# A hybrid DeltaNet, attention and FFN block: attention halves scaled in PSUM, decayed keys in 128-row tiles, FFN-down sums a stage ahead

## The chip, the cores and the metric

One core of a Trainium2 chip runs the whole program in one launch. The metric is the device time in microseconds (us), the median of several executions. The engines are named as in the profile: PE (TensorE matmul), PEld (its weight loads), DVE (VectorE), ACT (ScalarE), POOL (GpSimd), SP (SyncE, which issues the transfers).

## The reference

One layer on x of 1 x 1024 x 1024 (sequence, model width), all in float32:

```python
h = rmsnorm(x, norm_mix_w)
qa, ka, va, za, ba, aa, qb, kb, vb, ga, gb = split(h @ w_in)
# mixer A, 4 heads of 128: causal conv of 4 taps and SiLU on q, k, v, l2-norm of q and k,
# then per chunk of 64 positions, with G = cumsum(g), gam = exp(G):
w, uv = solve(I + beta*(k k^T)*dec_strict, [beta*gam*k, beta*v])   # unit lower triangular, 64 x 64
kd    = k * exp(G_last - G)                                        # decayed keys
def step(s, (w, uv, p, qg, kd, gl)):
    u = uv - w @ s
    o = qg @ s + p @ u
    s = gl * s + kd^T @ u                                          # state, 128 x 128
oa = rmsnorm(o) * silu(za)
# mixer B, 8 heads of 64: banded attention, a chunk sees itself and 8 chunks before, with relative bias
ob = softmax(0.125 * qb kb^T + bias) vb
x = x + (sigmoid(ga)*(oa @ w_branch_a) + sigmoid(gb)*(ob @ w_branch_b)) @ w_out
g, u = split(causal_dwconv3(rmsnorm(x) @ w_up) + b)                # 2 x 2816
out = rmsnorm(x + (silu(g)*u) @ w_down)
```

## The kernel before, in words

A float32 product is made of three faster ones (type fp32r): both operands are split into a high and a low half, and `hi*hi + hi*lo + lo*hi` are summed in PSUM. For weights `load_w` (L84) has SP load a tile `wraw`, ACT cast `whi` (L81) and POOL subtract `wlo` (L82). The normed input lies in SBUF as `BH` and `BL`. A *half* of a projection is 128 output channels by 512 positions: 8 k-tiles x 3 = 24 matmuls of 128x512 into one PSUM tile `psph`, all issued by `mm` (L52). There are two of these buffers (`psP`).

The stages follow each other: input norm and first projections (to about 60 us), DeltaNet (60 to 455), attention (455 to 745), mixing of the branches (745 to 845), `w_out` and the second norm (to 940), FFN up in Strassen-Winograd form (940 to 1350), FFN down in the same form, to the end.

DeltaNet, per head: `gdn_prep` (L400) transposes the keys into PSUM (`psk`), copies them to `nKs`, writes the decayed keys `Kd` (scaled by `eg[:, 2]`, L431) and sums squares (`jk`, `ssk`, L433, L434) for the norm `rk`. `gdn_prep2` (L441) makes the 64x64 matrices and scales `nKs` and `Vs` in place (L487, L488). The triangular system is solved in 31 steps on DVE (L506, L508) and its result, which goes through DRAM, is applied (`gdn_apply`, `psW`, `psU`, U). Then `gdn_chain` goes through 16 chunks, in 8 tiles p of two chunks e each:

```python
mm(ps, WQ[:, p, e * P:(e + 1) * P], S, start=True, stop=True)         # psws, 128 rows
nc.vector.tensor_add(U[r, p, :], ps[r], U[r, p, :])                   # r: rows of chunk e
mm(ps2, Kd[r, p, :], U[r, p, :], start=True, stop=True)               # pss, 64 rows
S2 = S * eg + ps2                                                     # DVE, L574
```

After each second chunk comes `pso`. These float32 matmuls take two passes each, and both stand in the trace as instructions. Projections of the next head and halves of the gates fill PE in between: the tables in L33 to L40 count, per head, how many tiles of the chain are emitted before which part of the next head (C1, C2, C3), how many halves go before `gdn_apply` and the q norm (APP, APK, QN), and how many gate halves are filled in (GFILL; 32 in all, 22 of them in DeltaNet). A scheduler then orders each engine's queue by priorities; `behind` puts work behind a named instruction.

A gate (`gate`, L166) takes two halves: DVE multiplies by the norm's factor into `gt`, ACT applies tanh, SP stores it. What is left of the gates after DeltaNet is woven into the last attention pair, 8 halves of it, and the rest runs behind it, ahead of the mixing. The mixing wants `oh`, `ol` (DeltaNet's output, from DRAM) and `bh`, `bl` (attention's, from `obT`), each cast by ACT and subtracted by DVE (`load_oa`, `split`).

Attention goes in four pairs of heads. `att_qkv` (L754) makes v, q and k in halves: `scaled` multiplies `psph` by the norm's factor into an SBUF tile `u` (two buffers, L768); ACT writes `Q` or `Kh` from it, DVE the low parts (`Q<-u,Q` L777, `Kl<-u,Kh` L787). v is transposed (`psvt`, in the same two PSUM buffers). `att_pair` makes scores (`pss`), softmax (`Sb`, `ast`), transposes (`psp`, `PTh`, `PTl`) and products with V (`pso`); each pair is woven with the projections of the next, the first pair's projections stand alone.

FFN up works on pairs of blocks with seven products P1 to P7 (`pa`, `pb`, `pc`, `pd` are PSUM tiles, `q` a sum in SBUF); DVE forms the sums that later products accumulate on (`sum_q`, `sum_pc`). FFN down goes through the seven products in the order P1, P5, P6, P3, P7, P2, P4, each 11 steps of 12 matmuls; `prep_w` (L1471) makes the weights of two steps at a time: DVE's sums `W<-W,W` for the two steps after, ACT's casts `wdh`, DVE's `wdl`; POOL or DVE splits the activations (`al`).

Of the kernel before, what the change touches and what calls it, by code (L numbers as in the profile page):

```python
# [8 lines left out]
F32 = mybir.dt.float32  # L9
# [26 lines left out]
APP = (10, 10, 10, 2)  # L36
APK = (7, 4, 3, None)
QN = (7, 3, 4, 5)
PR0 = 1
GFILL = (4, 4, 5, 5, 4)  # L40
# [6 lines left out]
def hybrid_kernel(ctx: ExitStack, tc: tile.TileContext, a):  # L47
# [176 lines left out]
    def first_rms(e):  # L224

        s = slice(e * HN, (e + 1) * HN)
        psr = psa.tile([P, HN], F32, tag="a", name="psrb")
        for i in range(4):
            xt = gp.tile([P, D], F32, tag=("Kd", "U")[i % 2], name="xt", bufs=2)
            nc.sync.dma_start(xt, a["x"][(4 * e + i) * P:(4 * e + i + 1) * P, :])  # L230
            ssq = sml.tile([P, 1], F32, tag="ssq", name="ssq")
            nc.scalar.activation(xt, xt, AF.Square, accum_out=ssq)
            ms = sml.tile([P, 1], F32, tag="ms", name="ms")
            nc.vector.tensor_scalar(out=ms, in0=ssq, scalar1=1.0 / D, scalar2=EPS, op0=ALU.mult, op1=ALU.add)
            rs = sml.tile([P, 1], F32, tag="rs", name="rs")
# [32 lines left out]
    wraw, whi, wlo = (gw.tile([P, KT, P], dt, tag=tg, name="wv") for dt, tg in ((F32, "sq"), (F32R, "nKs"), (F32R, "Vs")))  # L268
# [131 lines left out]
    def gdn_prep(c):  # L400
# [13 lines left out]
        Kd = gp.tile([P, NT, P], F32, tag="Kd", name="Kd", bufs=2)  # L414
# [8 lines left out]
        for e in range(2):  # L423
# [6 lines left out]
            for i in range(4):  # L430
                nc.scalar.activation(Kd[:, 4 * e + i, :], pks[e][:, i, :], AF.Copy, scale=eg[:, 2, 4 * e + i, h:h + 1])  # L431
            for i in range(4):
                nc.scalar.activation(jk, nKs[:, 4 * e + i, :], AF.Square, accum_out=ssk[:, 4 * e + i:4 * e + i + 1])  # L433
        nc.vector.tensor_scalar_add(ssk, ssk, EPS)  # L434
# [6 lines left out]
    def gdn_prep2(c):  # L441
# [19 lines left out]
        nc.scalar.activation(decT.rearrange("p n j -> p (n j)"), psd2, AF.Exp)  # L461
# [24 lines left out]
        for p in range(NT):  # L486
            nc.scalar.activation(nKs[:, p, :], nKs[:, p, :], AF.Copy, scale=nks[:, p:p + 1])  # L487
            nc.scalar.activation(Vs[:, p, :], Vs[:, p, :], AF.Copy, scale=bv[:, p:p + 1])  # L488
# [34 lines left out]
    def gdn_apply(c):  # L523
# [17 lines left out]
        U = gp.tile([P, NT, P], F32, tag="U", name="U", bufs=2)  # L541
# [14 lines left out]
    def gdn_chain(c):  # L556
# [6 lines left out]
        for p in range(NT):  # L563
            for e in range(2):
# [7 lines left out]
                mm(ps2, Kd[r, p, :], U[r, p, :], start=True, stop=True)  # L572
# [22 lines left out]
    def gdn_qnorm(c):  # L595

        sqq = gw.tile([P, NT, P], F32, tag="sq", name="sqq")
        nc.scalar.activation(sqq, c["WQ"][:, :, 64:192], AF.Square)
        psn = psc.tile([P, 8], F32, tag="c", name="psn")
        for p in range(NT):  # L600
            side.append(lambda p=p: mm(psn[:, p:p + 1], sqq[:, p, :], ones, start=True, stop=True))
        c["psn"] = psn
# [151 lines left out]
    def att_qkv(pr, c):  # L754
# [9 lines left out]
        def scaled(w, e):  # L764

            ps, s = proj_half(w, BH, BL, KT, e)
            u = ap_.tile([P, HN], F32, tag="u", name="u", bufs=2)
# [34 lines left out]
        for e in range(2):  # L802
            vT[e], s = scaled(w, e)
            yield
# [539 lines left out]
    prs[1].P2(True)  # L1344
    sub(BL[:, k1, s], b22, BH.bitcast(F32)[:, k1, s])
# [25 lines left out]
    p, r = prs  # L1371
    p.P5()
    p.sum_q()
    p.sum_pa()
    r.sum_pa()
    p.P6()
    p.sum_pc()
# [93 lines left out]
    def prep_w(k):  # L1471

        n = min(2, NS - 2 * k)
        for s in range(2 * k + 2, min(2 * k + 4, NS)):
            w_sum(s)
# [325 lines left out]
```

## Time and profile before

| | us |
|---|---|
| three runs | 1590.27, 1591.93, 1592.96 |
| median | 1591.93 |
| the profiled execution | 1592.53 |
| its span, first to last instruction | 1590.6 |
| PE busy | 1542.7 (97%) |
| DVE busy | 1120.3 (70%) |
| ACT busy | 698.0 (44%) |
| POOL busy | 595.6 (37%) |
| mean granted clock of PE | 0.994 |

Busy PE is a modelled figure for pipelined matmuls; what the tables below show as idle, with the instruction whose end released it, is the time in which PE had nothing to do. Operations of the FFN's helper all carry one line (L1155), so there the tiles tell them apart. In fp32r a projection matmul starts every 0.227 us at the full clock (2.4 GHz) and half as often at the lower level (1.2 GHz).

### The profile page before, as it was taken

The page shows a single profiled execution, that of the slowest core. Times are in us where ns is not written, and L with a number is a line of the kernel's source. Part 1 is how long each engine was busy: PE and PEld are TensorE (multiplying, and loading weights), DVE is VectorE, ACT ScalarE, POOL GpSimd, SP SyncE. Part 2 cuts the span into 40 slices and gives each one's busy share as a digit, 9 for nine tenths or more (in the row PEclk, how much of TensorE's full clock was granted, in tenths as well). Part 3 has the DMA queues.
Part 4 walks back from the last instruction along what each step waited for, and adds up shares of the span by engine and source line. Part 5 has one row for each costly group of instructions (what it writes and reads, how often), then busy time and mean ns, then how long its engine had stood idle before and what let it go on. Part 6 is the DMA issues. An engine that isn't in the chain of part 4 may idle for free.

```text
span 1590.6 us, 21158 instructions
## 1 busy us (share of the span) xinstructions
PE 1542.7 (97%) x7687; PEld 1255.8 (79%) x7687; DVE 1120.3 (70%) x2150; ACT 698.0 (44%) x1376; POOL 595.6 (37%) x449
## 2 busy tenths in 40 slices
PE   8999999999999999999999999999999999999997
PEld 6777776877777787888887887888888888788885
DVE  6795867948436878875665566777777777787787
ACT  7535334352225655654222244444444444433344
POOL 2422212212131101110220148877777776233353
PEclk9999999999999999999999999999999999999998
DMA  7021121122131101122654222233332332775533
GB/s 294 27 73 59 56 73 38 46 77 68 60 123 48 32 26 44 36 73 81 194 167 139 90 80 86 90 114 111 115 108 100 100 100 74 246 245 172 177 93 139
DMA packets 74504, 162.03 MB, mean 102 GB/s; under 512 B 15648, under 2 KB 16928, under 8 KB 74400
## 3 DMA queue, kind: packets, MB, share of 16 engines
q1 hardware_dynamic: 74400, 160.68, 30.5%
q8 instruction: 60, 0.98, 0.3%
q14 instruction: 44, 0.36, 0.1%
HBM read 120.55 MB, written 40.11 MB: 101 GB/s over the span
## 4 chain that ended last, share of the span: by engine, by line
PE 49%; DVE 3%; DMA 2%; ACT 1%; issue 1%; SPq 0%; POOL 0%; POOLq 0%; DVEq 0%; ACTq 0%
PE psph L52 8%; PE pb L52 7%; PE psd L52 7%; PE psout L52 5%; PE pc L52 5%; PE pa L52 4%; PE pb L1141 4%; PE psd L1493 3%; PE pc L1141 2%; PE pa L1141 2%; DMA araw<-dA 1%; DVE yu L1155 1%; PE pso L52 0%; DMA oaT<-dO 0%; DVE wdl L1155 0%
## 5 line engine op out<-in xcount | busy, mean ns | idle before, releaser
L82 POOL TENSOR_TENSOR wlo<-wraw,whi 128x1024 fp32r<-128x1024 f32 (+1 forms) x57 | 120.2, 2108 | 464.7 <-ACT whi L81 259.5
L52 PE MATMUL psph<-BH,whi 128*128 128x512 f32 x688 | 280.4, 408 | 10.1 <-ACT BH L220 5.2
L52 PE MATMUL psph<-BH,wlo 128*128 128x512 f32 x688 | 275.9, 401 | 1.7 <-POOL wlo L82 1.7
L52 PE MATMUL psph<-BL,whi 128*128 128x512 f32 x688 | 277.4, 403 | 0.0
L52 PEld LDWEIGHTS psph<-BH,whi 128*128 128x128 f32 x688 | 130.8, 190 | 34.8 <-ACT BH L220 5.9
L1155 POOL TENSOR_TENSOR ol<-wraw,oh 128x512 fp32r<-128x512 f32 x110 | 150.6, 1386 | 9.1 <-ACT oh L1155 9.1
L52 PEld LDWEIGHTS psph<-BH,wlo 128*128 128x128 f32 x688 | 130.8, 190 | 26.0 <-POOL wlo L82 2.1
L52 PEld LDWEIGHTS psph<-BL,whi 128*128 128x128 f32 x688 | 130.7, 190 | 23.1 <-DVE BL L221 1.0
L52 PE MATMUL psd<-wdl,ah 128*128 128x512 f32 (+1 forms) x311 | 121.6, 391 | 5.4 <-DVE wdl L1155 5.4
L1155 POOL TENSOR_TENSOR al<-araw,ah 128x1024 fp32r<-128x1024 f32 (+1 forms) x28 | 70.5, 2518 | 143.7 <-ACT ah L1155 143.6
L1155 POOL TENSOR_TENSOR wraw<-wraw 128x512 f32<-128x512 f32 x86 | 119.5, 1389 | 4.9
L1493 PE MATMUL psd<-wdh,al 128*128 128x512 f32 (+1 forms) x311 | 121.1, 390 | 0.0
L52 PE MATMUL psd<-wdh,ah 128*128 128x512 f32 (+1 forms) x311 | 119.8, 389 | 0.0
L1155 ACT CAST oh<-wraw 128x512 fp32r<-128x512 f32 x110 | 67.8, 621 | 102.0 <-POOL wraw L1155 101.9
L1155 DVE TENSOR_TENSOR wdl<-W,wdh 128x512 fp32r<-128x512 f32 x77 | 88.4, 1186 | 30.7 <-ACT wdh L1155 30.7
L1155 ACT CAST ah<-araw 128x1024 fp32r<-128x1024 f32 (+1 forms) x39 | 40.6, 1041 | 115.9 <-issue 48.8
L81 ACT CAST whi<-wraw 128x1024 fp32r<-128x1024 f32 (+2 forms) x61 | 55.4, 908 | 78.9 <-PE psph L52 55.1
L1155 POOL TENSOR_TENSOR gl<-wraw,gh 128x512 fp32r<-128x512 f32 x42 | 55.9, 1332 | 69.6 <-ACT gh L1155 69.6
L52 PEld LDWEIGHTS psd<-wdl,ah 128*128 128x128 f32 x311 | 58.8, 189 | 20.0 <-DVE wdl L1155 7.9
L1141 PE MATMUL pa<-BH,gh 128*128 128x512 f32 x176 | 68.6, 389 | 0.0
L52 PE MATMUL pa<-BH,gl 128*128 128x512 f32 x176 | 68.5, 389 | 0.0
L52 PE MATMUL pa<-BL,gh 128*128 128x512 f32 x176 | 68.5, 389 | 0.0
(342 smaller groups left out, 3826.2 us busy)
## 6 DMA issues: line engine op xcount, KB each, us to landing
wraw<-w_up SPq DMA_DIRECT2D x44, 512.0 KB, 4.9
wraw<-w_tiles SPq DMA_DIRECT2D x42, 512.0 KB, 3.5
araw<-dA SPq DMA_DIRECT2D x77, 256.0 KB, 3.0
dA<-yu SPq DMA_DIRECT2D x33, 512.0 KB, 3.1
W<-w_down SPq DMA_DIRECT2D x44, 256.0 KB, 4.7
xt<-x SPq DMA_DIRECT2D x16, 512.0 KB, 5.0
dG<-gt SPq DMA_DIRECT2D x16, 512.0 KB, 2.8
ta<-dG SPq DMA_DIRECT2D x16, 256.0 KB, 2.7
```

What stands on the lines that cost most here:

```text
L52: last["mm"] = nc.tensor.matmul(*args, **kw).ins
L81: nc.scalar.copy(hi, src)
L82: (eng or nc.gpsimd).tensor_tensor(out=lo, in0=src, in1=hi.bitcast(F32), op=ALU.subtract)
L1141: i = nc.tensor.matmul(ps, wh[:, k], xh[:, k], start=start and k == 0, stop=False, **kw)
L1155: return lambda *args, **kw: tc.keep_in_program_order(f(*args, **kw))
L1493: i = nc.tensor.matmul(ps, al[:, j, ts], wh[:, es], start=False, stop=stop, **kw)
```

## The change

Names and places (line numbers of before):

- `Kd` is a pair of persistent tiles [128, 8, 2, 128], zeroed by POOL at the start; the rows of chunk e lie in slot e, the other half stays zero. They are written in `gdn_prep2` from `nKs` instead of in `gdn_prep` from PSUM, as 16 ACT operations of 64 rows per head instead of 8 of 128 rows, and `pss` contracts all 128 rows.
- `ssk` gets its epsilon on POOL instead of DVE; some temporary tiles share other buffers.
- The tables APP, APK, QN and GFILL change: 24 gate halves in DeltaNet instead of 22.
- In attention q's and k's halves are scaled in place in `psph`; only v's go to `u`.
- At the FFN's start two products and their sums are emitted ahead of the last splits of the input.
- In FFN down the sums for P4 are made in the P2 stage.

```diff
-APP = (10, 10, 10, 2)
-APK = (7, 4, 3, None)
-QN = (7, 3, 4, 5)
+APP = (11, 10, 10, 2)
+APK = (2, 4, 3, None)
+QN = (7, 5, 7, 5)
 PR0 = 1
-GFILL = (4, 4, 5, 5, 4)
+GFILL = (6, 4, 5, 5, 4)
...
+    Kds = []
+    for i in range(2):
+        t_ = gp.tile([P, NT, 2, P], F32, name=f"Kd{i}")
+        nc.gpsimd.memset(t_, 0.0)
+        Kds.append(t_)
...
-        Kd = gp.tile([P, NT, P], F32, tag="Kd", name="Kd", bufs=2)
+        Kd = Kds[h % 2]
...
             nc.scalar.copy(nKs[:, 4 * e:4 * e + 4, :], pks[e])
             for i in range(4):
-                nc.scalar.activation(Kd[:, 4 * e + i, :], pks[e][:, i, :], AF.Copy, scale=eg[:, 2, 4 * e + i, h:h + 1])
-            for i in range(4):
                 nc.scalar.activation(jk, nKs[:, 4 * e + i, :], AF.Square, accum_out=ssk[:, 4 * e + i:4 * e + i + 1])
-        nc.vector.tensor_scalar_add(ssk, ssk, EPS)
+        nc.gpsimd.tensor_scalar_add(ssk, ssk, EPS)
...
-        nc.scalar.activation(decT.rearrange("p n j -> p (n j)"), psd2, AF.Exp)
+        last["exp"] = nc.scalar.activation(decT.rearrange("p n j -> p (n j)"), psd2, AF.Exp).ins
...
-        for p in range(NT):
-            nc.scalar.activation(nKs[:, p, :], nKs[:, p, :], AF.Copy, scale=nks[:, p:p + 1])
-            nc.scalar.activation(Vs[:, p, :], Vs[:, p, :], AF.Copy, scale=bv[:, p:p + 1])
+        Kd = c["Kd"]
+        with behind("exp"):
+            for p in range(NT):
+                for e in range(2):
+                    r = slice(e * CH, (e + 1) * CH)
+                    nc.scalar.activation(Kd[r, p, e, :], nKs[r, p, :], AF.Copy, scale=eg[r, 2, p, h:h + 1])
+                nc.scalar.activation(nKs[:, p, :], nKs[:, p, :], AF.Copy, scale=nks[:, p:p + 1])
+                nc.scalar.activation(Vs[:, p, :], Vs[:, p, :], AF.Copy, scale=bv[:, p:p + 1])
...
-        U = gp.tile([P, NT, P], F32, tag="U", name="U", bufs=2)
+        U = gp.tile([P, NT, P], F32, tag="U", name="U")
...
-                mm(ps2, Kd[r, p, :], U[r, p, :], start=True, stop=True)
+                mm(ps2, Kd[:, p, e, :], U[:, p, :], start=True, stop=True)
...
-        def scaled(w, e):
+        def scaled(w, e, out=False):
             ps, s = proj_half(w, BH, BL, KT, e)
-            u = ap_.tile([P, HN], F32, tag="u", name="u", bufs=2)
+            u = ap_.tile([P, HN], F32, tag="u", name="u", bufs=2) if out else ps
             nc.vector.tensor_mul(u, ps, rb[:, s])
             return u, s
...
-            vT[e], s = scaled(w, e)
+            vT[e], s = scaled(w, e, True)
...
     prs[1].P2(True)
+    p, r = prs
+    p.P5()
+    p.sum_q()
+    p.P6()
+    p.sum_pc()
     sub(BL[:, k1, s], b22, BH.bitcast(F32)[:, k1, s])
     sub(hf[:, k1], hf[:, k1], tf[:, k1])
     vsplit(hf[:, k1], BH[:, k0, s], BL[:, k0, s])
...
-    p, r = prs
-    p.P5()
-    p.sum_q()
     p.sum_pa()
     r.sum_pa()
-    p.P6()
-    p.sum_pc()
     p.gate_a()
...
         for s in range(2 * k + 2, min(2 * k + 4, NS)):
-            w_sum(s)
+            if plan[s // FH][0] == "P2":
+                w_sum(s + FH)
+            elif plan[s // FH][0] != "P4":
+                w_sum(s)
```

PE in the first pair of attention, behind the second `psvt`: before (its next `psph` is the second half of q).

```order
L52 MATMUL psph<-BH,wlo 128x512
L792 MATMUL psvt<-ident,u 128x128 [waits DVE_49,PE_49]
L792 MATMUL psvt<-ident,u 128x128 x3
L52 MATMUL psph<-BH,whi 128x512 [waits DVE_49]
L52 MATMUL psph<-BL,whi 128x512
```

The same place now.

```order
L52 MATMUL psph<-BH,wlo 128x512
L802 MATMUL psvt<-ident,u 128x128 [waits DVE_49]
L802 MATMUL psvt<-ident,u 128x128 x3
L52 MATMUL pss<-Kh_4358,Q_4356 128x256 [waits Activation_49]
L52 MATMUL pss<-Kh_4358,Q_4356 128x256
L52 MATMUL pss<-Kl_4360,Q_4356 128x256 [waits DVE_49]
L52 MATMUL pss<-Kl_4360,Q_4356 128x256
L52 MATMUL psph<-BH,whi 128x512 [waits DVE_49,PE_49]
```

Four scores moved ahead of that half, and its first matmul now waits for PE's and DVE's work on the half that used the buffer before.

PE at the end of the last attention pair, before: the last gate half (`BH`), then the first half of the mixing, whose `oh` of k-tile 3 and `bh` are cast last.

```order
L52 MATMUL psph<-BH,wlo 128x512
L52 MATMUL psph<-oh_6420,whi 128x512 [waits DVE_49]
L52 MATMUL psph<-ol_6421,whi 128x512
L52 MATMUL psph<-oh_6420,wlo 128x512 [waits Pool_49]
L52 MATMUL psph<-oh_6426,whi 128x512
L52 MATMUL psph<-ol_6427,whi 128x512
L52 MATMUL psph<-oh_6426,wlo 128x512
L52 MATMUL psph<-oh_6432,whi 128x512
L52 MATMUL psph<-ol_6433,whi 128x512
L52 MATMUL psph<-oh_6432,wlo 128x512
L52 MATMUL psph<-oh_7177,whi 128x512 [waits Activation_49]
L52 MATMUL psph<-ol_7178,whi 128x512 [waits DVE_49]
```

The same place now, right behind the last `pso` of the pair.

```order
L52 MATMUL pso<-PTl_4351,V 128x256
L52 MATMUL psph<-oh_6504,wlo 128x512
L52 MATMUL psph<-oh_6510,whi 128x512
L52 MATMUL psph<-ol_6511,whi 128x512
L52 MATMUL psph<-oh_6510,wlo 128x512
L52 MATMUL psph<-oh_7193,whi 128x512 [waits Activation_49]
L52 MATMUL psph<-bh_7199,whi 128x512 [waits Activation_49]
L52 MATMUL psph<-ol_7194,whi 128x512 [waits DVE_49]
L52 MATMUL psph<-oh_7193,wlo 128x512
L52 MATMUL psph<-bl_7203,whi 128x512 [waits DVE_49]
L52 MATMUL psph<-bh_7199,wlo 128x512 [waits Pool_49]
L52 MATMUL psph<-bh_7200,whi 128x512 [waits Activation_49]
```

No gate half stands between the last `pso` and the mixing any more, and the first two halves of the mixing take turns.

DVE at the FFN's start, before.

```order
L1155 TENSOR_TENSOR XT3l<-tf,XT3h 128x4x128 [waits Activation_49]
L1155 TENSOR_TENSOR BL<-pst,BH 128x4x128
L1155 TENSOR_TENSOR hf<-hf,tf 128x512
L1155 TENSOR_TENSOR BL<-hf,BH 128x4x128 [waits Activation_49]
L1155 TENSOR_TENSOR q<-pc,p_8611 128x512 [waits PE_49]
L1155 TENSOR_TENSOR pa<-pa,p_8611 128x512
L1155 TENSOR_TENSOR pa<-pa,p_8700 128x512
L1155 TENSOR_TENSOR pc<-pb,q 128x512 [waits DVE_49,PE_49]
```

The same place now.

```order
L1165 TENSOR_TENSOR XT3l<-tf,XT3h 128x4x128 [waits Activation_49]
L1165 TENSOR_TENSOR q<-pc,p_8627 128x512 [waits PE_49]
L1165 TENSOR_TENSOR pc<-pb,q 128x512 [waits DVE_49,PE_49]
L1165 TENSOR_TENSOR BL<-pst,BH 128x4x128
L1165 TENSOR_TENSOR hf<-hf,tf 128x512
L1165 TENSOR_TENSOR BL<-hf,BH 128x4x128 [waits Activation_49]
L1165 TENSOR_TENSOR pa<-pa,p_8627 128x512
L1165 TENSOR_TENSOR pa<-pa,p_8716 128x512
```

`q` and `pc` moved ahead of `BL`, `hf`, `BL` and the two `pa`.

## Rows read from the trace of the kernel before

**Rows 1.** Page, part 1: busy us and share of the span by engine.

```profile
PE 1542.7 (97%) x7687; PEld 1255.8 (79%) x7687; DVE 1120.3 (70%) x2150; ACT 698.0 (44%) x1376; POOL 595.6 (37%) x449
```

**Rows 2.** Windows in DeltaNet: us, busy time (x instructions) by engine, granted clock, DMA share, GB/s.

```profile
160.00:180.00 20.00, 19.49 (x92) 14.11 (x91) 17.26 (x42) 5.74 (x14) 3.25 (x6) 1.00 0.17 53
415.00:455.00 40.00, 39.09 (x187) 28.20 (x186) 22.81 (x63) 8.53 (x25) 5.66 (x3) 1.00 0.11 40
```

**Rows 3.** Instruction groups, PE, 60 to 460: count, busy, mean ns, idle before.

```profile
L52 PE MATMUL pss<-U,Kd 64*128 64x128 f32 x128 | 31.6, 327 | 4.5 <-DVE U L569 4.5
L52 PE MATMUL psws<-S,WQ 128*128 128x128 f32 x128 | 25.5, 281 | 1.4 <-DVE S L574 1.4
```

**Rows 4.** Timeline, PE, chain of the first head: start, us, line, matmul, tile.

```profile
176.88 0.39 PE L52 MATMUL psph<-BL,whi 128*128 128x512 f32 x1
177.12 0.38 PE L52 MATMUL psws<-S,WQ 128*128 128x128 f32 x2
...
177.57 0.40 PE L52 MATMUL psph<-BH,whi 128*128 128x512 f32 x1
177.81 0.40 PE L52 MATMUL psph<-BL,whi 128*128 128x512 f32 x1
178.13 0.48 PE L52 MATMUL pss<-U,Kd 64*128 64x128 f32 x2
...
178.88 0.39 PE L52 MATMUL psph<-BH,whi 128*128 128x512 f32 x1
```

**Rows 5.** Timeline, DVE, the same chain.

```profile
174.95 0.29 DVE L569 TENSOR_TENSOR U<-psws,U 64x128 f32<-64x128 f32 x1
...
176.22 0.34 DVE L574 SCALAR_TENSOR_TENSOR S<-S,eg,pss 128x128 f32<-128x128 f32 x1
...
177.54 0.28 DVE L569 TENSOR_TENSOR U<-psws,U 64x128 f32<-64x128 f32 x1 [0.48 <-PE psws L52]
```

**Rows 6.** Instruction groups, ACT, 60 to 455.

```profile
L431 ACT ACTIVATE Kd<-psk,eg 128x128 f32<-128x128 f32 x32 | 10.1, 390 | 0.0
```

**Rows 7.** Timeline, ACT and DVE, end of attention.

```profile
747.36 3.91 ACT L81 CAST bh<-obT 128x1024 fp32r<-128x1024 f32 x4
...
748.52 3.50 DVE L82 TENSOR_TENSOR bl<-obT,bh 128x1024 fp32r<-128x1024 f32 x3 [0.72 <-ACT bh L81]
```

**Rows 8.** Timeline, DVE and POOL, a woven pair of attention.

```profile
552.41 0.55 DVE L867 TENSOR_TENSOR PTl<-psp,PTh 128x384 fp32r<-128x384 f32 x1
552.88 1.94 DVE L787 TENSOR_TENSOR Kl<-u,Kh 64x512 fp32r<-64x512 f32 x1
...
554.91 0.69 DVE L787 TENSOR_TENSOR Kl<-u,Kh 64x512 fp32r<-64x512 f32 x1
...
551.86 2.41 POOL L82 TENSOR_TENSOR wlo<-wraw,whi 128x1024 fp32r<-128x1024 f32 x1 [9.40 <-PE psp L862]
```

**Rows 9.** Timeline, PE in attention: rows with idle time and its releaser.

```profile
499.77 0.33 PE L862 MATMUL psp<-ident,Sb 128*128 128x128 f32 x1 [1.70 <-DVE Sb L851]
...
544.43 0.76 PE L862 MATMUL psp<-ident,Sb 128*128 128x128 f32 x5 [1.78 <-DVE PTl L867]
```

**Rows 10.** Timeline, first pair: PE where k's and q's halves begin, ACT's copies.

```profile
476.30 0.47 PE L52 MATMUL psph<-BH,whi 128*128 128x512 f32 x1 [0.87 <-DVE u L768]
...
482.78 0.50 PE L52 MATMUL psph<-BH,whi 128*128 128x512 f32 x1 [0.35 <-DVE u L768]
...
484.80 0.62 ACT L786 CAST Kh<-u 64x512 fp32r<-64x512 f32 x1
```

**Rows 11.** FFN start: timeline of PE, and window 960 to 970.

```profile
962.27 0.50 PE L1141 MATMUL pb<-XT3h,oh 128*128 128x512 f32 x1 [2.11 <-DVE pc L1155]
...
960.00:970.00 10.00, 7.89 (x28) 6.22 (x28) 6.41 (x10) 4.39 (x7) 8.47 (x8) 0.83 0.50 154
```

**Rows 12.** Timeline, PE and DVE, last stage of down.

```profile
1567.51 0.50 PE L52 MATMUL psd<-wdl,ah 128*128 128x512 f32 x1 [2.45 <-DVE wdl L1155]
...
1563.37 3.48 DVE L1155 TENSOR_TENSOR W<-W,W 128x512 f32<-128x512 f32 x2
```

More of the change, by code (lines that the diff above doesn't have):

```diff
@@ L228, in first_rms @@
         for i in range(4):
-            xt = gp.tile([P, D], F32, tag=("Kd", "U")[i % 2], name="xt", bufs=2)
+            pool, tag = ((gp, "U"), (gp, "Lr"), (gw, "vf"))[i % 3]
+            xt = pool.tile([P, D], F32, tag=tag, name="xt")
             nc.sync.dma_start(xt, a["x"][(4 * e + i) * P:(4 * e + i + 1) * P, :])
@@ L267, in hybrid_kernel @@
     nc.vector.tensor_scalar_mul(nea, nea, -1.0)
-    wraw, whi, wlo = (gw.tile([P, KT, P], dt, tag=tg, name="wv") for dt, tg in ((F32, "sq"), (F32R, "nKs"), (F32R, "Vs")))
+    wraw, whi, wlo = (gw.tile([P, KT, P], dt, tag=tg, name="wv") for dt, tg in ((F32, "kf"), (F32R, "nKs"), (F32R, "Vs")))
     nc.sync.dma_start(wraw, a["w_tiles"][2 * GH])
@@ L595, in gdn_qnorm @@
     def gdn_qnorm(c):
-        sqq = gw.tile([P, NT, P], F32, tag="sq", name="sqq")
+        sqq = gp.tile([P, NT, P], F32, tag="zs", name="sqq")
         nc.scalar.activation(sqq, c["WQ"][:, :, 64:192], AF.Square)
```

## The prediction

> **What bounds the kernel now.** I read the page's busy shares first, then the granted clock by stretch, then what ends TensorE's idle time, and last the timelines around those places. TensorE (PE) is busy 97% of the span, VectorE (DVE) 70% [rows 1]: so the time is PE's work plus PE's holes, and an edit counts only if it takes passes from PE, closes a hole, or opens one. The profiled execution took 1592.53 us for a span of 1590.6; it lies 0.6 us above the median of the runs, 1591.93. I make the sum against 1592.5 and take 0.6 off at the end. A change of under 0.2% (3.2 us) can hardly be told from none here.
>
> In DeltaNet PE is nearly full (19.49 of 20 us, 39.09 of 40), but DVE is not far behind in some stretches: 17.26 of 20 us at 160 to 180, only 22.81 of 40 in the last head [rows 2].
>
> **Decayed keys in 128 rows.** The state update `pss` contracts 64 rows before, 128 after (the other 64 are zeros). Its passes have the longest mean of the chain, 327 ns against 281 for `psws`, which has the same 128 columns and contracts 128 rows [rows 3]. The timeline tells more. From one projection matmul at 176.88 to the second one after it, at 177.57, with a `psws` pair between them, are 0.69 us; from 177.81 to 178.88, with a `pss` pair between, 1.07 us [rows 4]. Without a pair two projection steps take 2 x 0.23 = 0.46. So a `psws` pair costs PE 0.23 and a `pss` pair 0.61: the change of shape costs time going in and coming out. There are 128 `pss` passes, 64 pairs: 64 x 0.38 = **24.3 us** is the most that can go. The Trainium skill ("TensorEngine Tiling (Array Packing)", When to Use Tiling) advises row tiling for a contraction of 64, which speaks against this edit; its Key Properties add that a switch of mode drains the engine, and that is what these rows show for a lone tile among full ones. By the first rule alone this edit would save nothing.
>
> How much of 24.3 survives? The chain is a loop PE, DVE (U), PE, DVE (S). Its step is 2.59 us from one U to the next [rows 5]. The loop's own time I estimate at 1.7 us: the `psws` pair 0.38 + U 0.28 + the `pss` pair about 0.45 + S 0.34 + some 0.25 for four hand-overs [rows 4, 5]. A step shortened by 0.38 is 2.2, so the loop itself does not bind, and in all chains PE waited for U only 4.5 us and for S 1.4 [rows 3]. But where DVE is busy 17.26 of 20 us [rows 2], taking seven steps x 0.38 = 2.7 us out leaves it no air, and each U or S then stands behind somebody's 0.7 us operation. I take **-18** (bounds 0 and -24.3; the value lies nearer the upper end, since the last head has a DVE at 57% [rows 2] and the small waits for U and S speak for room in the others).
>
> **Preparing a head.** Eight ACT copies per head, 390 ns each [rows 6], go from the path to `ssk`, and sixteen come in later, behind the exponential of `decT`. ACT has room; what can suffer is a conv activation queued behind the now 32-long block (about 0.39 x 16 = 6 us more at worst, of which the fill hides all but 0 to 2 us a head). The sum of `ssk` moves to POOL, which then no longer waits for DVE's queue; nothing of PE hangs on that. The two zero fills on POOL at the start lie before its first work. The renamed buffers I cost at nothing: U of the next head is written after the previous chain has ended. Together **-1** (from -2.5 to +4).
>
> **Gate halves.** Two gate halves (48 matmuls, 10.9 us of PE at 0.227) move from behind the last attention pair into DeltaNet. As work they cost the same. But there they were cover: they ran while ACT cast the four `bh` (3.91 us) and DVE made the `bl` (3.50 for three) [rows 7]. In the changed order PE has 4 matmuls left after the last `pso` and then wants `oh`, `bh`, `ol`, `bl` in turn. ACT needs about 1.0 us each, DVE 1.17 for `ol` and each `bl`, starting one cast later: 0.6 + 1.0 + 5 x 1.17 + 0.5 = 7.9 us until the last is used, against 19 matmuls x 0.227 = 4.3. What is late next is `bl`: **+3.5** (0 to +6).
>
> **Queries and keys in PSUM.** Gain: DVE's Q and Kl operations read two SBUF operands now. `Kl` takes 1.94 us while POOL computes `wlo` (2.41 us, from 551.86), and 0.69 after it [rows 8]; `PTl`, in the middle of the same `wlo` but with an operand in PSUM, takes 0.55. So with `psph` in place of `u` I expect about 0.7 beside POOL too. The price of it now is PE waiting for what DVE does next: 1.78 us at 544.43 [rows 9]. Three such holes of 1.8 (one a woven pair), three of about 1.1 behind the second of k's halves, and one of 1.70 in the first pair make 10.3 us. The Trainium skill ("VectorE: DVE Perf Modes", Rules for kernel authors) would copy to SBUF first when many operations follow; the rows (0.55 and 0.69 with either source) give no reason to.
>
> Cost: the accumulator is held until its last reader. There are two such buffers, shared with `psvt`. In the first pair, where nothing is woven in, k's first half follows q's first half on the same buffer. Today it starts at 476.30 after 0.87 idle [rows 10]. The idle time began at 475.43, behind a `psvt` of about 0.6, so q's last matmul ends near 474.8. After: hand-over 0.2, scaling 0.69, one copy for Q, one for V and one more for Q on ACT (0.62, some 0.4, 0.62) and DVE's last Q 0.69 make 478.0: +1.7. The second half of q waits for four ACT copies (0.62 each, the last from 484.80) and the last Kl: about 3.0 idle in place of 0.35 [rows 10], +2.7. In woven pairs the scores, transposes and value products of the pair before lie between the halves, and I add 1.5 for all of it, half-clock stretches included. Together -10.3 + 4.4 + 1.5 = **-4.4** (from -10 to +8).
>
> **FFN start.** `q` and `pc` come ahead of three other operations on DVE. Now PE waits 2.11 us for `pc`, and the granted clock of the ten microseconds from 960 is 0.83 [rows 11]: 10 x 0.17 = 1.7 us lost to the lower level (1.2 of 2.4 GHz) after that hole. `pc` can be ready 2 to 3 us sooner, both should go: **-3.5** (-3.8 to 0; the displaced BL is then late by some tenths).
>
> **Down.** The sums for P4 move a stage ahead. PE's hole of 2.45 us ends at 1567.51 on a `wdl` that stood behind two sums, 3.48 us [rows 12]; a part stays, since `wdl` itself has two SBUF operands beside POOL's `al`. The P2 stage now has these sums, in front of its own `wdl`: where a pair falls beside POOL's work it costs 3.48 there too, and a new hole of 1 to 2 us is likely. **-3** (-5 to +1).
>
> **Sum:** -18 - 1 + 3.5 - 4.4 - 3.5 - 3 = -26.4; 1592.5 - 26.4 = 1566.1, less 0.6: **1565.5 us**; with the spread of the terms 1557 to 1573.
>
> **Rivals.** (1) *DVE takes over in the chains.* For: the 17.26 of 20 us. Against: 5.9 us of waits for U and S in four heads. Then 18 shrinks to about 8: 1575.5 (1573 to 1583). Chance 0.15. (2) *Held accumulators (slower).* Place: each half of k and the second half of q, two a pair, eight waits. Should the woven work not cover them either, each costs 3.0 us of idle and the 1.7 us of lower clock that followed a hole of 2.1: 8 x 4.7 = 38, and the -10.3 is not seen. The other terms give -22, so it decides from 2.75 us a wait on; at 4.7 the time is 1592 - 22 + 38 = 1608 (1595 to 1610). Against: PE's rows between the halves in woven pairs. Chance 0.05. (3) *128 rows cost what 64 do,* because the passes next to them, not the shape, make the 0.61: no saving in the chains, 1583.5. The rule on row tiling of the skill's page would have it so. Against: `psws` in the same neighbourhood. Chance 0.06, with 0.03 of it within 0.2% when the holes stay as well. (4) *All holes close and the chains give the full 24:* 1550 to 1557. Chance 0.16.
>
> **How the numbers follow.** The forecast's own case has 0.55, rival 1 0.15, rival 2 0.05, rival 3 0.06, rival 4 0.16, and 0.03 stays for other losses around 1585. The range 1553 to 1580 leaves out rivals 2 and 3, the ends of 1 and 4: under 0.2. Faster: 0.92; same 0.03; slower 0.05.
>
> **What would show it.** Right: `pss` as a 128*128 pass with a mean near 280 ns, and two projection steps around it in 0.69; PE's work in DeltaNet shorter by some 14 us net of the added halves; Q and Kl at about 0.7 each; no wait for `pc` at the FFN's start and a clock of 1.0 behind it. Wrong: PE idle before `pss` or `psws` summing to over 15 us (rival 1), PE idle before `psph` in woven pairs with Kl or Q as releaser (rival 2), `pss` still at 0.6 a pair (rival 3). New holes I expect at k's and q's halves in the first pair, before `bl`, and in P2.

## The result and the profile after

The changed kernel takes 1574.3 us (median of four runs, 1572.72 to 1575.6), the kernel before 1592.33 in the runs beside it. The ratio is 0.9889, interval 0.9871 to 0.9906: 18 us faster, inside the range, 8.8 us above the forecast. The profiled execution took 1573.87 us, its span is 1572.1 (before: 1590.6).

Where the 18.5 us of span went, by the first or last matmul of a kind in both traces (us from the span's start; each length is the difference of two marks):

| stretch, up to | before | changed | length before | length changed | difference |
|---|---|---|---|---|---|
| last `psoT` (DeltaNet ends) | 458.29 | 448.54 | 458.29 | 448.54 | -9.75 |
| first `psvt` | 474.83 | 465.05 | 16.54 | 16.51 | 0.0 |
| last `pso<-PT` (attention ends) | 746.65 | 738.69 | 271.82 | 273.64 | +1.82 |
| first `psout` (mixing ends) | 844.32 | 828.78 | 97.67 | 90.09 | -7.58 |
| last `psout` | 939.20 | 923.54 | 94.88 | 94.76 | -0.12 |
| first matmul with `XT3` | 962.27 | 944.37 | 23.07 | 20.83 | -2.24 |
| first `psd` (down begins) | 1361.14 | 1342.05 | 398.87 | 397.68 | -1.19 |
| last `psd` | 1582.61 | 1564.10 | 221.47 | 222.05 | +0.58 |
| end | 1590.59 | 1572.08 | 7.98 | 7.98 | 0.0 |

The first row runs from the start of the span. DeltaNet's own stretch, from the first `psdec` (at 62.70 before, 61.13 now) to the last `psoT`, fell from 395.6 to 387.4 us. DeltaNet took in 10.9 us of gate work and the mixing stage lost as much, so in their own terms DeltaNet gained 19.1 us and the end of attention lost 3.3. The 1.6 us ahead of DeltaNet were not forecast, and no run here shows where they come from. In shares of the span PE and DVE are as busy as in [rows 1]:

```profile
PE 1526.2 (97%) x7687; PEld 1247.6 (79%) x7687; DVE 1108.7 (71%) x2146; ACT 713.0 (45%) x1408; POOL 598.2 (38%) x455
```

The chain's groups, as in [rows 3], and three rows of its timeline that answer to [rows 4]:

```profile
L52 PE MATMUL psws<-S,WQ 128*128 128x128 f32 x128 | 27.0, 293 | 2.0 <-DVE S L584 1.9
L52 PE MATMUL pss<-U,Kd 128*128 128x128 f32 x128 | 26.1, 285 | 7.4 <-DVE U L579 7.3
```

```profile
170.19 0.40 PE L52 MATMUL psph<-BL,whi 128*128 128x512 f32 x1
170.43 0.38 PE L52 MATMUL pss<-U,Kd 128*128 128x128 f32 x2
...
170.88 0.39 PE L52 MATMUL psph<-BH,whi 128*128 128x512 f32 x1
```

`pss` passes fell from 327 to 285 ns, and from the projection matmul ahead of a pair to the second one behind it are 0.69 us, as around `psws`, in place of 1.07. PE's waits for U grew from 4.5 to 7.3 us. DVE's share of the window that stood at 17.26 of 20 us [rows 2] did not grow:

```profile
160.00:180.00 20.00, 19.05 (x102) 14.69 (x101) 15.14 (x49) 11.28 (x33) 3.07 (x4) 1.00 0.18 57
```

But a share of 15 of 20 does not mean that U starts at once. Of the 9.4 us that PE idles ahead of `pss` and `psws`, DVE works for 6.5 on something else than U or S (before: 3.9 of 5.9). Here U stands behind `zs`, which itself had waited for ACT:

```profile
354.33 0.69 DVE L601 SCALAR_TENSOR_TENSOR zs<-zth,zs 128x512 f32<-128x512 f32 x1 [1.40 <-ACT zth L600]
355.05 0.29 DVE L579 TENSOR_TENSOR U<-psws,U 64x128 f32<-64x128 f32 x1
355.40 0.49 PE L52 MATMUL pss<-U,Kd 128*128 128x128 f32 x2 [1.23 <-DVE U L579]
```

Attention: DVE's groups (the former means are 1125 and 1032 ns; one of the slow Kl stands in [rows 8]), and PE's waits, answering to [rows 9, 10]:

```profile
L787 DVE SCALAR_TENSOR_TENSOR Q<-psph,Q 64x512 fp32r<-64x512 f32 x16 | 11.0, 689 | 2.1 <-ACT Q L786 1.7
L797 DVE TENSOR_TENSOR Kl<-psph,Kh 64x512 fp32r<-64x512 f32 x16 | 11.0, 688 | 5.7 <-ACT Kh L796 5.4
```

```profile
467.89 0.47 PE L52 MATMUL psph<-BH,whi 128*128 128x512 f32 x1 [2.24 <-DVE V L808]
...
475.61 0.50 PE L52 MATMUL pss<-Kh,Q 128*128 128x256 f32 x2 [1.55 <-ACT Kh L796]
...
529.88 0.50 PE L52 MATMUL psph<-BH,whi 128*128 128x512 f32 x1 [1.19 <-DVE Kl L797]
```

The seven holes (idle times of PE) before transposes are gone. In their place stand two in the first pair and one of 1.19 in each of three woven pairs, all before a `psph` or a score that waits for what ACT and DVE read out of these two PSUM buffers. Behind the second hole of the first pair the granted clock is at its lower level for a while, which the kernel before does not show anywhere in attention:

```profile
475.00:485.00 10.00, 9.17 (x33) 7.28 (x34) 4.11 (x14) 4.13 (x9) 0.00 (x0) 0.83 0.00 0
```

Such a half-clock stretch costs some 1.6 us when it comes singly: about eight projection matmuls start every 0.43 us in it (in the kernel before at 963.78, 964.20 and 964.63), so not quite half as often as the 0.227 us at the full clock.

The end of attention: PE waits, and DVE makes `bl` in one row behind the other [rows 7]:

```profile
740.50 0.50 PE L52 MATMUL psph<-oh,whi 128*128 128x512 f32 x1 [0.59 <-ACT oh L81]
741.45 0.50 PE L52 MATMUL psph<-bh,whi 128*128 128x512 f32 x1 [0.44 <-ACT bh L81]
742.89 0.62 PE L52 MATMUL psph<-bl,whi 128*128 128x512 f32 x1 [0.41 <-DVE bl L82]
...
741.62 4.62 DVE L82 TENSOR_TENSOR bl<-obT,bh 128x1024 fp32r<-128x1024 f32 x4
```

The FFN's start: no wait ahead of `XT3`, and the full clock [rows 11]:

```profile
944.37 0.39 PE L1151 MATMUL pb<-XT3h,oh 128*128 128x512 f32 x1
...
943.00:953.00 10.00, 9.74 (x43) 7.74 (x42) 7.22 (x10) 6.43 (x10) 9.90 (x9) 1.00 0.40 114
```

FFN down: PE's waits (the 2.45 of [rows 12] is gone, four others stand there), then SP's queue and ACT at the end:

```profile
1517.89 0.50 PE L52 MATMUL psd<-wdl,ah 128*128 128x512 f32 x1 [1.71 <-DVE wdl L1165]
1546.33 0.50 PE L52 MATMUL psd<-wdl,ah 128*128 128x512 f32 x1 [0.85 <-DVE wdl L1165]
1554.69 0.50 PE L52 MATMUL psd<-wdh,ah 128*128 128x512 f32 x1 [1.48 <-ACT wdh L1165]
1556.06 0.79 PE L52 MATMUL psd<-wdl,ah 128*128 128x512 f32 x1 [0.87 <-DVE wdl L1165]
```

```profile
1548.16 2.07 SPq L1165 DMA_DIRECT2D out_dram<-ot  x2
1550.34 0.37 SPq L1165 DMA_DIRECT2D araw<-dA  x1
...
1553.50 0.62 ACT L1165 CAST ah<-araw 128x512 fp32r<-128x512 f32 x1 [3.39 <-DMA araw<-dA]
```

The last activation load is issued behind two output stores that wait for DVE's `ot`; ACT idles 3.39 us for it, and PE for ACT.

### The profile page after: what moved, and what is told of

It is laid out like the page before. It is cut to its first block, busy times and chain, and to the rows that moved or that the text cites. A ratio compares the mean times of both kernels' runs of the same rounds, so it can differ in the third digit from the quotient of the medians.

```text
span 1572.1 us, 21179 instructions
## 1 busy us (share of the span) xinstructions
PE 1526.2 (97%) x7687; PEld 1247.6 (79%) x7687; DVE 1108.7 (71%) x2146; ACT 713.0 (45%) x1408; POOL 598.2 (38%) x455
## 4 chain that ended last, share of the span: by engine, by line
PE 49%; DVE 3%; issue 2%; DMA 1%; ACT 1%; SPq 0%; POOL 0%; POOLq 0%; DVEq 0%; ACTq 0%
PE psph L52 8%; PE pb L52 7%; PE psd L52 6%; PE psout L52 5%; PE pa L52 5%; PE pc L52 5%; PE pb L1151 4%; PE psd L1506 3%; PE pa L1151 2%; PE pc L1151 2%; DMA araw<-dA 1%; DVE wdl L1165 1%; DVE yu L1165 1%; PE pso L52 1%; SPq L1165 0%
## 5 line engine op out<-in xcount | busy, mean ns | idle before, releaser
L52 PEld LDWEIGHTS psd<-wdl,ah 128*128 128x128 f32 x311 | 58.8, 189 | 19.2 <-DVE wdl L1165 7.5
L52 PEld LDWEIGHTS psd<-wdh,ah 128*128 128x128 f32 x311 | 58.7, 189 | 14.1 <-ACT wdh L1165 1.9
```

The source lines that it names most:

```text
L52: last["mm"] = nc.tensor.matmul(*args, **kw).ins
```

## The experiments

All start from the changed kernel and edit one place. Ratios are to the kernel before, in runs on the same chip; for the changed kernel it is 0.9889 (0.9871 to 0.9906). Edits of a few us are told by the stretch that they touch, since the intervals of the whole overlap. A stretch comes from one profiled execution, and kernels that have the same code in it show how far it moves by itself: DeltaNet (first `psdec` to last `psoT`) 387.3 to 390.9 us, attention (first `psvt` to last `pso`) 273.2 to 275.6, down (first to last `psd`) 221.1 to 222.9. Half-clock stretches, present in some of these traces and not in others, make part of that spread.

**Does the shape of `pss` cost the time?** The tiles keep their zeros, the matmul takes 64 rows again.

```diff
-                mm(ps2, Kd[:, p, e, :], U[:, p, :], start=True, stop=True)
+                mm(ps2, Kd[r, p, e, :], U[r, p, :], start=True, stop=True)
```

> The changed kernel with one edit: pss contracts the 64 rows of its chunk again, from the same zero-padded tiles and with all else as changed. Theory (the change of shape costs 0.38 us of PE a pair, and the chains kept most of it): pss back to some 325 ns a pass, DeltaNet 18 to 24 us longer, run 1592 to 1598. Rival (128 rows cost what 64 do, the gain in DeltaNet came from the moved copies and tables): DeltaNet within 3 us of the changed kernel, run 1572 to 1577. Rival (DVE limits the chains anyway): DeltaNet only 8 to 12 us longer, because waits for U and S shrink by as much as the passes grow, run 1582 to 1587.

Measured: 1589.74 us, ratio 0.9995 (0.9984 to 1.0005), DeltaNet 14.7 us longer (402.1 against 387.4, from the first `psdec` to the last `psoT`). The groups and the timeline in this kernel:

```profile
L52 PE MATMUL pss<-U,Kd 64*128 64x128 f32 x128 | 31.1, 322 | 4.1 <-DVE U L579 4.1
L52 PE MATMUL psws<-S,WQ 128*128 128x128 f32 x128 | 24.9, 276 | 1.5 <-DVE S L584 1.5
```

```profile
171.90 0.40 PE L52 MATMUL psph<-BL,whi 128*128 128x512 f32 x1
172.23 0.48 PE L52 MATMUL pss<-U,Kd 64*128 64x128 f32 x2
...
172.98 0.39 PE L52 MATMUL psph<-BH,whi 128*128 128x512 f32 x1
```

1.08 us around the pair, with everything else as in the changed kernel, where it is 0.69: the shape alone makes the 0.39. So the rival that 128 rows cost the same falls. The 14.7 lie between the theory's 18 to 24 and the last rival's 8 to 12.

Of 64 x 0.38 = 24.3 us, 22.1 are there when the steps around all 64 pairs are added up without the idle time; where a `pso` follows the pair, a pair gives 0.33. PE's idle time in DeltaNet is 3.8 us smaller here than in the changed kernel (10.9 against 14.7), nearly all of it in waits for U and S (4.1 + 1.5 against 7.3 + 1.9), and `psws` passes are shorter (276 against 293 ns, 2.1 us in 128): when `pss` gets cheaper, the chain's loop through DVE takes part of it back. The last 1.5 us were not told apart. Counted without the gate work, this kernel's DeltaNet is 4.4 us shorter than that of the kernel before (402.1 against 395.6 + 10.9): that is what everything but the shape is worth there. Part of it is two half-clock stretches of the kernel before, where this one has none in DeltaNet:

```profile
255.00:265.00 10.00, 8.24 (x34) 5.98 (x33) 5.75 (x13) 0.81 (x4) 1.10 (x1) 0.83 0.36 115
370.00:380.00 10.00, 8.64 (x33) 5.68 (x31) 7.58 (x23) 1.13 (x5) 2.35 (x1) 0.83 0.33 105
```

In the Trainium skill ("TensorEngine Tiling (Array Packing)", Key Properties) a change of mode drains the engine; the 1.08 against 0.69 agrees. The advice there to tile the rows of a short contraction (When to Use Tiling) does not hold for a lone tile among full matmuls: here it costs 14.7 us.

**What do the moved copies do?** `Kd` is written in `gdn_prep` again, now in sixteen operations; the later loop loses them.

```diff
+                for ee in range(2):
+                    rr = slice(ee * CH, (ee + 1) * CH)
+                    nc.scalar.activation(Kd[rr, 4 * e + i, ee, :], pks[e][rr, i, :], AF.Copy, scale=eg[rr, 2, 4 * e + i, h:h + 1])
...
-                for e in range(2):
-                    r = slice(e * CH, (e + 1) * CH)
-                    nc.scalar.activation(Kd[r, p, e, :], nKs[r, p, :], AF.Copy, scale=eg[r, 2, p, h:h + 1])
```

> The changed kernel with one edit: Kd is written from psk in the preparation again, as sixteen operations of 64 rows there, and the later block is 16 long as before. Theory (the moved copies cleared the path to the matrices of the decays: the holes of 0.9 us behind Kd, of 1.7 behind wlo and of 0.7 behind gih in the kernel before): holes there return, DeltaNet 2 to 6 us longer than 387.4, run 1576 to 1580. Rival (these holes went with the tables or the order, not with the copies): DeltaNet within 1 us.

Measured: 1578.69 us, ratio 0.9924 (0.9908 to 0.9941), DeltaNet 5.1 us longer (392.5). PE's idle rows, and what DVE does ahead of the second:

```profile
69.53 0.47 PE L52 MATMUL psd<-gsh,mleR 128*128 128x512 f32 x1 [0.88 <-ACT Kd L440]
...
89.01 0.47 PE L52 MATMUL psph<-BH,whi 128*128 128x512 f32 x1 [4.66 <-DVE tmp L517]
...
345.19 0.50 PE L52 MATMUL psd<-gsh,mleR 128*128 128x512 f32 x1 [2.34 <-ACT Kd L440]
```

```profile
81.99 6.16 DVE L387 SCALAR_TENSOR_TENSOR acc<-u,prm,acc 128x512 f32<-128x512 f32 x6 [6.08 <-ACT acc L385]
```

The interval does not overlap the changed kernel's, and 392.5 lies 1.6 above the longest of the kernels with the same DeltaNet: the place of the copies is worth more than the 1 us forecast, but not all of the 5.1 is the path through `Kd`. Two of the holes end on `Kd`, 3.2 us in sum. The third and longest ends on DVE, which had waited 6.08 us for a convolution on ACT and then did six of its operations in a row; the kernel before has no hole of that length in DeltaNet. Behind this hole and the one at 345 stands a half-clock stretch each, and the changed kernel has none in DeltaNet. With the eight copies of before the cost is smaller: there one hole of 0.91 us ends on `Kd`.

**Was the gate work cover, or needed as fill?** The tables APP, APK and GFILL of before, QN as changed.

```diff
-APP = (11, 10, 10, 2)
-APK = (2, 4, 3, None)
+APP = (10, 10, 10, 2)
+APK = (7, 4, 3, None)
-GFILL = (6, 4, 5, 5, 4)
+GFILL = (4, 4, 5, 5, 4)
```

> The changed kernel with the tables APP, APK and GFILL of before (22 gate halves in DeltaNet, 10 left for the last pair); QN stays as changed. Theory (the two halves covered the casts of bh and bl at the end of attention): the three holes before oh, bh and bl (1.4 us idle in sum, some 3.7 us of time with what they stretch) go; the 10.9 us of PE move out of DeltaNet, which gets shorter by 8 to 11; run 1569 to 1573. Rival (DeltaNet needs the two halves as fill): DeltaNet shrinks by less than 6 us, since its holes grow, run 1576 or more.

Measured: 1578.31 us, ratio 0.9921 (0.9905 to 0.9937). The three holes at the end of attention are gone: from the last `pso` to the first `psout` 97.42 us, 86.5 without the 10.9 of gate work, against 90.09. So the lost cover costs 3.6 us. But DeltaNet, with 10.9 us less to do, takes 387.8 us, as long as with it:

```profile
148.14 0.49 PE L52 MATMUL pss<-U,Kd 128*128 128x128 f32 x2 [1.88 <-DVE U L579]
...
171.10 0.49 PE L52 MATMUL psws<-S,WQ 128*128 128x128 f32 x2 [1.46 <-DVE S L584]
...
185.53 0.98 PE L644 MATMUL psoT<-ident,O 128*128 128x128 f32 x3 [1.52 <-ACT O L636]
...
220.00:240.00 20.00, 19.17 (x141) 15.71 (x140) 7.08 (x16) 6.27 (x14) 2.39 (x1) 0.83 0.30 93
```

In the changed kernel none of these holes is there. In DeltaNet PE idles 4.5 us longer than in the changed kernel (19.2 against 14.7), and half-clock stretches from 148.7, 186.2 and 230.6, the last of them twice as long as the others, cost some 6.4 more; the row from 220 to 240 shows the last one at 0.83. Together that is the whole 10.9. Two of the stretches stand right behind holes shown here, the third behind a wait of 0.81 us for a transfer. So the first head's chain, once `pss` is cheap, has too little beside it. In these two profiles the span is 6.3 us longer without the two halves there, although the end of attention gains 3.6. By the medians the run is 4.0 longer; the two fastest of its four runs (1576.33 and 1576.49) are 0.7 us or more above the slowest of the changed kernel, so a loss stays, but how much of the 6.4 of lower clock each run has is not known.

**Attention.** Three edits: q and k both through SBUF again; k alone; or two of k's four copies taken from `Kh` in place of `psph`.

```diff
-            u = ap_.tile([P, HN], F32, tag="u", name="u", bufs=2) if out else ps
+            u = ap_.tile([P, HN], F32, tag="u", name="u", bufs=2)
```

> The changed kernel with one edit: the halves of q and k are scaled into the SBUF tile u again, as before. Theory (the held accumulators gave back what the faster Q and Kl operations won): Q and Kl go back to means of 1.1 and 1.0 us beside POOL, PE's waits at the transposes come back (about 10 us) and those of psph for Kl go (about 8 us and one half-clock stretch), attention from its first psvt to its last pso 271 to 275 us against 273.6, run within 3 us of 1574. Rival (attention lost time to the new order, not to held accumulators): the waits of psph stay, run 1580 or more. Rival (holding is a plain loss): run 1569 or less.

Measured: attention (first `psvt` to last `pso`) 271.84 us against 273.64 and against 271.82 before; run 1572.25, ratio 0.9885 (0.9871 to 0.99). Q and Kl are back at 1125 and 1032 ns, the holes too, and the half-clock stretch of the first pair is gone. What the change gained in attention it gave back.

```diff
         def k_half(w, e):
-            ps, s = scaled(w, e)
+            ps, s = scaled(w, e, True)
```

> The changed kernel with one edit: k's halves go through the SBUF tile u again, q's stay in PSUM. Theory (holding costs where k's half is followed at once by q's; q's own low parts gain): waits of psph for Kl go (3 x 1.2), the wait before a transpose behind Kl beside POOL comes back (3 x 1.1), the one behind Q does not; attention 269 to 273 us against 273.6 with all in PSUM and 271.8 with all in SBUF. Rival: it is the first pair alone that loses, so woven pairs stay as they are and attention is 271 to 272.

Measured: 269.79 us, run 1570.3, ratio 0.9871 (0.9856 to 0.9886). Of the 3.85 us against the changed kernel 1.4 are idle time (7.7 against 9.0) and some 1.6 the half-clock stretch of the first pair, which is not there. In this kernel Q is fast, Kl slow, and the hole behind Kl is smaller than it was (0.88 now, 1.1 before):

```profile
L797 DVE TENSOR_TENSOR Kl<-u,Kh 64x512 fp32r<-64x512 f32 x16 | 16.8, 1053 | 1.6 <-ACT Kh L795 1.2
L787 DVE SCALAR_TENSOR_TENSOR Q<-psph,Q 64x512 fp32r<-64x512 f32 x16 | 11.0, 689 | 2.0 <-ACT Q L786 1.6
```

```profile
547.17 0.55 PE L872 MATMUL psp<-ident,Sb 128*128 128x128 f32 x3 [0.88 <-DVE PTl L877]
```

That PSUM operands free DVE from POOL agrees with the Trainium skill ("SBUF — State Buffer", Who interferes with whom: an operation with two SBUF inputs contends with a GpSimd instruction that reads SBUF, one with at most one input there does not); 1125 and 689 ns are the numbers for it here.

```diff
                 nc.scalar.copy(Kh[j][r, s], ps[r])
-                nc.scalar.copy(Kh[j][x, s], ps[r])
                 nc.vector.tensor_tensor(out=Kl[j][r, s], in0=ps[r], in1=Kh[j].bitcast(F32)[r, s], op=ALU.subtract)
+            for j in range(2):
...
+                nc.scalar.copy(Kh[j][x, s], Kh[j].bitcast(F32)[r, s])
```

> The changed kernel with one edit: of the four copies of a half of k, the two into the other 64 rows read Kh in SBUF, behind the two that read psph; so the accumulator is free after two copies and two Kl, not four and two. Theory (the held accumulator is what PE waits for): the three waits of 1.2 us for Kl in woven pairs and the one of 1.55 in the first pair shrink by 0.6 to 1.2 each, attention (first psvt to last pso) 268 to 271.5 us against 273.6. Rival (DVE's own queue makes Kl late): waits unchanged within 0.3 us, attention 273 to 275.

Measured: 272.82 us, run 1571.86, ratio 0.9885 (0.987 to 0.99). In the woven pairs the wait falls from 1.19 to 0.54, three times, as the theory has it; in the first pair the scores now wait longer for the late copy:

```profile
478.51 0.39 PE L52 MATMUL pss<-Kh,Q 128*128 128x256 f32 x1 [1.97 <-ACT Kh L800]
...
531.31 0.50 PE L52 MATMUL psph<-BH,whi 128*128 128x512 f32 x1 [0.54 <-DVE Kl L796]
```

The stretch as a whole missed the 268 to 271.5 and lies close to the kernels with unchanged attention. This trace has two half-clock stretches in the first pair, one more than the changed kernel's; without them it would be at some 269.6 against 272.0, an estimate from the 1.6 us each.

**FFN down.** The sums back in P4 (the condition replaced by `w_sum(s)`); the sums four steps sooner still; the last load issued ahead of the stores.

> The changed kernel with one edit: the sums for P4 are made in the P4 stage again. Theory (the moved sums opened a hole of 1.7 us in the P2 stage, closed the one of 2.5 us in P4, and the last activation load then ended last): the P2 hole goes back to 0.9, a hole of about 2.5 us is back in P4, the two holes at the very end (1.5 and 0.9 us) shrink, and FFN down takes as long within 1.5 us; run 1572 to 1576. Rival (the move did gain and only the lower clock hid it): FFN down 3 us longer, run 1577. Rival (it lost): FFN down 2 us shorter, run 1572 or less.

Measured: 220.85 us for down against 222.05, run 1573.16, ratio 0.9892 (0.9876 to 0.9909). Holes of 0.89, 0.52, 2.45, 0.34 and 0.43 us in the places of 1.71, 0, 0.85, 1.48 and 0.87: moved, not removed. The 1.2 us between the two lie within what down varies by itself: a half-clock stretch at 1555.5 stands in the changed kernel's down, behind the hole of 1.48, and none in this one's.

```diff
-            if plan[s // FH][0] == "P2":
-                w_sum(s + FH)
-            elif plan[s // FH][0] != "P4":
+            if plan[s // FH][0] != "P4":
                 w_sum(s)
+            if 6 * FH <= s + FH + 4 < NS:
+                w_sum(s + FH + 4)
```

> The changed kernel with one edit: the sums for P4 run four steps sooner still, so that the last of them lies ahead of POOL's products in the P2 stage. Theory (the P2 hole of 1.7 us is sums beside POOL): that hole goes below 1.0, the hole of 0.9 in P4 and the two at the very end (1.5 and 0.9) stay or grow; FFN down 220 to 221.5 us against 222.05. Rival (wdl itself, not the sums, is late in P2): hole stays at 1.5 or more.

Measured: 221.22 us, run 1573.62, ratio 0.9896 (0.9879 to 0.9912). The P2 hole of 1.71 is gone altogether, and the end waits as long as before, 1.67 and 0.87. The 0.8 us that down lost are within its spread.

```diff
             prep(k + 1)
+            if s + 7 == NS:
+                a_load(k + 3)
```

The general condition for loads then leaves out this last one.

> The changed kernel with one edit: SP issues the load of the last activation block ahead of the last two output stores instead of behind them. Theory (the end waits for this load, which stands behind stores that wait for DVE): it is issued some 4 us sooner, the hole of 1.5 us for wdh goes and the one of 0.9 behind it shrinks; FFN down 219.5 to 220.7 us against 222.05. Rival (the ring of buffers, not SP's order, sets its time): issue within 1 us of before, hole unchanged.

Measured: 218.80 us, run 1571.12, ratio 0.9883 (0.9867 to 0.99). SP issues all three loads in one go, and the wait for `wdh` is gone; of the two at the end one of 0.68 is left:

```profile
1543.80 2.12 SPq L1165 DMA_DIRECT2D araw<-dA  x3
1548.01 2.07 SPq L1165 DMA_DIRECT2D out_dram<-ot  x2
```

Of the 3.25 us that down gains, 1.7 are the holes at the end and some 1.6 the half-clock stretch behind them, which is gone; against the shortest of the kernels with unchanged down, 221.1, the gain is 2.3.

**FFN start.** P5, its sum, P6 and `pc` back behind the splits, as the lines with a minus in the diff of the change.

> The changed kernel with one edit: at the FFN's start P5, its sum, P6 and pc come behind the last splits again. Theory (the earlier pc closes a hole of 2.1 us and with it a stretch at half clock): the wait of PE for pc of about 2.1 us is back and a half-clock stretch of 3.4 us behind it; the time from the first w_out product to the first product of down 3 to 4 us longer than 513.3; run 1577 to 1579. Rival (the clock falls for another reason): the hole alone, 2.2 us, run 1576 or less.

Measured: 1577.42 us, ratio 0.9912 (0.9892 to 0.9932). The wait is back and the stretch is 2.2 us longer (23.03), but the clock does not fall:

```profile
947.00 0.50 PE L1151 MATMUL pb<-XT3h,oh 128*128 128x512 f32 x1 [2.05 <-DVE pc L1165]
...
945.00:955.00 10.00, 8.00 (x35) 6.64 (x36) 6.14 (x10) 4.72 (x7) 9.76 (x9) 1.00 0.54 160
```

So the rival's reading holds in this stretch: the edit is worth the hole of 2.2 us, and the time from the first `w_out` product to the first of down is 515.1 against 513.3, below the theory's 3 to 4. The lower clock in the trace of before did not have to follow; one trace of each does not tell how often it does. The median is 3.1 us above the changed kernel's, inside the theory's range of 1577 to 1579, with intervals that overlap; in the profiled execution the rest of the difference lies far from the edit, most of it in down (0.9 us).

**A version that beats both.** k through SBUF, in the first pair q too (`scaled(w, e, pr == 0)`), the sums four steps sooner, the last load sooner.

> The changed kernel with k's halves (and in the first pair q's too) through the SBUF tile u, the P4 sums four steps sooner and the last activation load ahead of the last two stores. Theory (the three gains are in different places and add): attention 268 to 270 us against 273.6, FFN down 217.5 to 218.8 against 222.05, run 1564 to 1568. Rival (a hole closed at the end is opened by the next late load or weight): down 219 or more, run 1569 or more.

Measured: 1566.04 us, ratio 0.9837 (0.982 to 0.9855), an interval wholly below the changed kernel's; attention 268.49, down 217.18. Neither of the two has a half-clock stretch. Then one of the `bh`, `bl` pairs is made ahead of the last weave:

```diff
+            bh0, bl0 = (mwa.tile([P, T], F32R, name=f"b{x}0") for x in "hl")
+            split(obT[:, 0, :], bh0, bl0, nc.vector)
...
```

> The kernel best with one edit more: the first of the four bh, bl pairs is made ahead of the last weave, in the room that the earlier queries and keys leave. Theory (the casts and subtractions at the end of attention are late there by one operation each): the mixing stage 0.9 to 1.3 us shorter than 90.1 to 91.0. Rival (the wait moves to the other bh): within 0.4 us.

Measured: 1563.62 us, ratio 0.983 (0.9812 to 0.9848); the mixing stage 89.09 against 90.05. The medians are 2.4 us apart with intervals that overlap, so the edit itself is shown by the 1.0 us of its stretch. Of the waits at the end of attention the one for `oh` is gone, those for `bh` and `bl` remain:

```profile
736.09 0.51 PE L52 MATMUL psph<-bh,whi 128*128 128x512 f32 x1 [0.45 <-ACT bh L81]
737.54 0.50 PE L52 MATMUL psph<-bl,whi 128*128 128x512 f32 x1 [0.40 <-DVE bl L82]
```

## Why the prediction was right or wrong

- **Decayed keys and preparation**, forecast -18 and -1: DeltaNet gained 19.1 us against its work. The sum was right, its split was not: the shape gives 14.7, all else in DeltaNet 4.4. In that rest are the holes on the way to the matrices of the decays, of which the copies are one cause, and two half-clock stretches of the kernel before, at 257 and 373 us, some 1.6 each, where the changed one has none; that the sum came out so close is in part luck. The tables APK and QN and the sum of `ssk` on POOL were not tried alone. Rival 1 named DVE as what would take the rest, with U and S behind somebody's operation; that is what the longer waits show, but they are 3.6 us of the shape's 22.1 and not half, and DVE's share of the window fell from 17.26 to 15.14.
- **Gate halves**, forecast +3.5: at the end of attention 3.3 by the marks, 3.6 by the experiment, so that price was right. Missed: "As work they cost the same." In DeltaNet they cost nothing: without them the stretch is as long, by 4.5 us of idle time and 6.4 of lower clock in that trace. As a whole the move was a gain and not a loss, of 4.0 us by the medians of a run that turns the three tables back together.
- **Queries and keys in PSUM**, forecast -4.4, measured +1.8: the step that failed. The gain was as told (all seven holes, 10.2 us, Q and Kl at 689 and 688), and the first pair cost 2.6 us in holes over those it had, where 4.4 was forecast. The step "In woven pairs the scores, transposes and value products of the pair before lie between the halves, and I add 1.5 for all of it, half-clock stretches included" was mis-sized: three waits of 1.19, one half-clock stretch behind the first pair's holes, some 1.6, and PE is busy some 3.4 us longer for the same 1455 matmuls in another order, in steps under 0.3 us. The prediction did not look for that last part, and it was not traced further. That all of it came with the held halves and the order that goes with them is shown by the run that takes them back: 271.84 us, as before. Rival 2 named this mechanism; it came at five places, with 7.4 us of idle time and one half-clock stretch, about a quarter of its 38.
- **FFN start**, forecast -3.5, measured -3.4 (2.24 + 1.19): right in sum; the first part is the edit's, but that the second, the lower clock, goes with the hole is not shown, since in the experiment it stayed at 1.00 with the hole there.
- **Down**, forecast -3, measured +0.6: the P2 hole came as told (0.89 grew to 1.71), the one in P4 shrank by 1.6. What was missed is the end: "a part stays" looked for a late `wdl`, but what is late next is a load in SP's queue. The forecast counted SP's queue nowhere.
- The range held; rival 1's time, 1575.5, was the closest, for another reason. The two terms that were too good, 6.2 us in attention and 3.6 in down, are the miss; the 1.6 us ahead of DeltaNet, which nobody forecast, made it smaller.

## What to carry to other kernels

A contraction of 64 rows alone between full matmuls cost 0.39 us a pair more here than the same with zero rows added; look for such lone shapes in a chain. An accumulator that is worked on in place is a buffer held: count the time to its last reader against the work between two uses, pair by pair. When a wait closes, look at every queue for what is late next, the loads behind stores in particular; and before calling moved work neutral, ask which side has idle time.

## What the runs showed that was not expected

The lower clock does not follow a hole of a given length in these traces. After an idle time of 2.11 us ahead of `XT3` the granted clock fell to half (0.83 over ten microseconds), after 2.05 at the same place in another kernel it stayed at 1.00. Ahead of the first pair's k half ten kernels (the changed one and nine of its edits) have a hole of 2.24 or 2.25 us: the clock fell behind it in three (those with 64 rows in `pss`, with the copies back, and with two copies from `Kh`). Nine of these ten have a second hole some 8 to 10 us later, of 1.55 to 1.97 us, and there it fell in all nine.

In three kernels that differ from the changed one only far behind DeltaNet (with q and k in SBUF, with two copies from `Kh`, and the first of the better versions) the profiled execution shows half-clock stretches at 62 and 76 us and DeltaNet 1.9 to 3.5 us longer; no cause for it was found in the edits.
